# Where two joining copies of an encoder's FFN stand on ScalarE's queue: ahead of a weight cast, or behind it

## The chip, the cores and the metric

The kernel runs on one core of a Trainium2 chip. The time is that of the whole program on the device in microseconds (us), the median of several executions. A core has a matrix engine (TensorE, PE), three engines for elementwise work (VectorE or DVE, ScalarE or ACT, GpSimd or POOL), and SyncE (SP), which issues most of the DMAs here. Each engine has its own list of instructions, and the lists are tied by semaphores.

## The reference

Two layers (`DEPTH`) work on 256 tokens of width 1024. Each layer has a mixing part (gated linear attention and grouped-query attention in parallel, merged and projected), a SwiGLU FFN, and a per-layer embedding. The change concerns the FFN alone:

```python
D_MODEL = 1024
SEQ = 256
FFN_HIDDEN = -(-8 * D_MODEL // (3 * 256)) * 256      # 2816
...
    gate, up = jnp.split(rms_norm(h, g_ffn_pre) @ w_ffn_in, 2, axis=-1)
    h = h + rms_norm((jax.nn.silu(gate) * up) @ w_ffn_out, g_ffn_post)

    e = p_i @ w_ple_proj
    h = h + rms_norm(jax.nn.sigmoid(h @ w_ple_gate) * e, g_ple_post)
```

All inputs are float32.

## The kernel before, in words

**Precision.** A float32 matrix product is made of three products in the type fp32r: each operand is split into a high part (a cast on ScalarE) and a low part (the rest, a subtraction on VectorE). `split` (L135) issues both, the cast first. So every weight that TensorE uses costs a ScalarE cast and a VectorE subtraction, in two halves of 128x1024 each, and VectorE's half needs ScalarE's.

**Weights.** `Stream` (the object `ws`) brings the weights, in units of 128x2048 float32. SP's queue issues a load (L298) into a buffer `raw_…` (there are two), the split goes into a pair `wh_…`, `wl_…` (four of each), and TensorE frees a pair with the last matmul that reads it. `put` cuts a unit into two halves; `fill` splits ordinary units, `made` those of a pair (below).

**The order of the FFN.** The hidden 2816 columns are 11 blocks of 256. The first block is done by halves of the tokens; three (`PLAIN`, 4, 5 and 10) are done plainly; three pairs of blocks (`PAIRS` = 2, 6, 8) are done by seven products in place of eight (`seven`, with the weight sums of `step` on VectorE in buffers called `lent_…`). A string says in which order the parts come: u is half a plain block, 1 to 7 are the products of a pair, o is one step of the projection back (`out_step`), p loads a gain:

```python
FFN = "uu12u34u5u67" "uo12o34o5o67" "poo12o345o67"
PLAIN, PAIRS = (4, 5, 10), (2, 6, 8)
OUT = (0, 1, 2, 3, 4, 5, 10, 6, 7, 8, 9)
```

TensorE's order follows this string. The steps behind it (`out_step` for the eleven blocks, the product with the embedding's gate) make up the layer's end.

**Turning the hidden activations.** The projection back needs them with the hidden index on the partitions. `turned` does this as a task in the background for each half of the tokens (`hf` 0 or 1) of the first block and of each pair, and once for a plain block. `turn_out` (L456) copies the two 16-bit planes of the activations apart on ScalarE (L461 or L466) and has SP issue a transposing DMA (L467); some matmuls later, `take_in` (L470) joins the planes with a copy on ScalarE (L474, the "joining copy", a tile `mid_…` from a tile `t_…`) and splits the result into `hid` (a tile `big_…`): a joining cast on ScalarE and a joining low part on VectorE. The last pair is turned on TensorE instead.

**Who sets the order on the queues.** A scheduler gives each engine its list; work from a piece of code that stands earlier has priority, and `tc.high_priority(AHEAD)` lifts some of it. `tc.issue_after(x.ins)` holds what is issued in it behind the instruction `x`. Before the change, `take_in` used it for one copy alone: that of (k, hf) = (0, 0), behind the copy apart of (0, 1).

**The other neighbours.** `gain` (L373) loads a gain row for all partitions through SP, `up_weights` (L828 to L832) loads and casts the small decay weights of the next layer, and in `seven` the copies L738, L741 and L745 take products from PSUM.

Of the kernel before, what the change touches and what calls it, by code (L numbers as in the profile page):

```python
# [43 lines left out]
PLAIN, PAIRS = (4, 5, 10), (2, 6, 8)  # L44
# [17 lines left out]
def trunk_kernel(ctx: ExitStack, tc: tile.TileContext, a: dict, out: bass.AP):  # L62
# [28 lines left out]
    def mid(dt=F32):  # L91
        return b4p.tile([P, 1024], dt, tag="mid", name=nm("mid"))
# [40 lines left out]
    def split(hi, lo, src):  # L133

        return nc.scalar.copy(hi, src), nc.vector.tensor_tensor(out=lo, in0=src, in1=hi.bitcast(F32), op=ALU.subtract)  # L135
# [99 lines left out]
    class Load:  # L235


        def __init__(self, make, own=None, waits=False):
            self.make, self.own, self.waits, self.raw, self.n = make, own, waits, None, 0
# [8 lines left out]
    class Stream:  # L248
# [7 lines left out]

        def __init__(self, depth):
            self.depth, self.held, self.room, self.ready, self.open = depth, 0, 0, [], False
            self.loads, self.jobs, self.lend, self.last = [], [], False, {}
            pairs = {}  # L260
            for item in plan:
                if callable(item):
                    x = Load(item)
                    self.loads.append(x)
                    self.jobs.append(lambda x=x: self.plain(x))
                else:
                    units, n = item
                    if n == 1:
                        b11, b12, b21, b22 = units
                        x, z = (Load(b, lambda tag=tag: self.lent(tag), tag == "wh") for b, tag in ((b11, "wh"), (b12, "wl")))  # L270
                        y, q = Load(b22, big), Load(b21)
                        pairs[id(units)] = x, y, z, q
                        self.loads += [x, y, z]
                    if n == 5:
                        self.loads.append(q)
                    self.jobs.append(lambda p=pairs[id(units)], n=n: self.step(n, *p))
# [41 lines left out]

        def made(self, x):
            for piece in self.put(x):  # L320
                split(*piece)

        def step(self, n, x, y, z, q):
            c = slice(0, 2048)
# [22 lines left out]
        def fill(self):  # L347
            while self.open and self.held < self.depth and self.jobs:
                n = self.total - len(self.jobs)
                pieces = self.jobs.pop(0)()  # L350
                for piece in pieces or ():
                    self.last[n] = split(*piece)
                if pieces:
                    self.load()

# [12 lines left out]
    ws = Stream(4)  # L368
# [77 lines left out]
    def transpose_in(sp, src, k, n, hf, plain=None):  # L446

        ps = aux()
        for i in range(n):
            nc.tensor.transpose(ps[:, i * P : (i + 1) * P], src[:, i * P : (i + 1) * P], ident)  # L450
        with tc.high_priority(AHEAD):
            sp.put(ps[:, : n * P], k, n, hf * P, P)
        if plain is not None:
            nc.scalar.copy(plain, ps[:, : n * P])

    def turn_out(src, parts, mixed=False):  # L456

        with tc.high_priority(AHEAD):
            planes, words = (t.bitcast(U16) for t in (parts, src))
            if mixed:  # L460
                apart = nc.scalar.copy(  # L461
                    planes.rearrange("p (s k h f) -> p s k h f", s=2, k=2, f=P),
                    words.rearrange("p (h k f s) -> p s k h f", h=2, f=P, s=2),
                )
            else:
                apart = nc.scalar.copy(planes.rearrange("p (s c) -> p s c", s=2), words.rearrange("p (c s) -> p s c", s=2))  # L466
        nc.sync.dma_start_transpose(out=words.rearrange("p (x t) -> p x t", t=P), in_=planes)  # L467
        return apart

    def take_in(hi, lo, src, parts, behind=None):  # L470

        tn = hi.shape[-1]
        with tc.issue_after(behind.ins) if behind is not None else nullcontext():
            nc.scalar.copy(  # L474
                parts.bitcast(U16).rearrange("p (k t s) -> p k t s", s=2, t=tn),
                src.bitcast(U16).rearrange("p (s k t) -> p k t s", s=2, t=tn),
            )
        split(hi, lo, parts.rearrange("p (k t) -> p k t", t=tn))

    last_pow = [None]  # L480

# [62 lines left out]
    def halves(t):  # L544
        return [t[:, j * 512 : (j + 1) * 512] for j in range(2)]
# [140 lines left out]
    def sums(x):  # L686

        made = []

        def make():
            yield 1
            (a11, a12), (a21, a22) = x() if callable(x) else x
            s2 = t512()
            vsub(a22, a21, a22)
            vsub(s2, a11, a22)
            vsub(a12, a12, s2)  # L700
            yield 1
            vsub(a21, a21, a11)
            for s in (a12, a22, a21, s2):
                parts = halves(mid(F32R))
                split(*parts, s)
                made.append([p.rearrange("p (k t) -> p k t", t=P) for p in parts])
                yield 1

        return made, Task(make(), part[0])

    def seven(sp, forms, gated, alone=()):

        made, task = forms
        quad = lambda hf, j: lambda k: sp.tok(4 * j + k, hf)
        form = lambda i: lambda k: [p[:, k, :] for p in made[i]]
# [286 lines left out]
    def keep_embedding():  # L1002

        made = next(embedding)
        kept = keptp.tile([P, 2, D], F32, tag="kept", name=nm("kept"))
        nc.sync.dma_start(kept, made)
        return kept
# [39 lines left out]
    for l in range(DEPTH):  # L1047
# [249 lines left out]
        for x in range(2):  # L1297
            for i, o in enumerate(project_t(uT)):
                dst, r = qk[:, x, i, :], 1.0 if x else P**-0.5
# [142 lines left out]
        for j in range(2):  # L1442
            o = project(uT)
            for hf in range(2):
                dst = gg[:, hf, j * 512 : (j + 1) * 512]
# [3 lines left out]
        def out_gate():  # L1449
            while not (gla.over and attention.over):  # L1450
                yield 1
            for hf in range(2):
                sg = mid()
                with tc.issue_after(last_exp[0].ins):
                    nc.scalar.activation(sg, gg[:, hf, :], AF.Sigmoid)
                for j, t in enumerate(halves(sg)):
                    s = slice(j * 512, (j + 1) * 512)
                    vmul(t, t, gg[:, hf, s])
                    vmul(t, t, on[:, hf, s])
                xs = [(t, gg[:, hf, j * 512 : (j + 1) * 512]) for j, t in enumerate(halves(sg))]  # L1460
                for x in xs:
                    turn_out(*x)

                def turn(hf=hf, xs=xs):
                    for j, x in enumerate(xs):
                        yield WAIT_GATED[hf] if j == 0 else 1
                        take_in(*gT.at(4 * j, 4, hf * P, P), *x)

                gT.makers[hf].append(Task(turn(), part[0]))
# [107 lines left out]
        hid, spare, apart = Split(), [], {}  # L1577
        us = [[ws.take() for _ in range(2)] for _ in range(2)]

        def turned(src, k, hf):  # L1580

            def turn():
                if k == 2 * PAIRS[-1]:
                    yield WAIT_LAST[hf]
                    transpose_in(hid, src, k, 4, hf)
                else:
                    if not spare:
                        spare.extend(halves(mid()))
                    parts = spare.pop()
                    apart[k, hf] = turn_out(src, parts, hf is None)  # L1590
                    yield WAIT_TURNED
                    while (k, hf) == (0, 0) and (0, 1) not in apart:
                        yield 1
                    dst = hid.at(k, 2, 0, T) if hf is None else hid.at(k, 4, hf * P, P)
                    take_in(*dst, src, parts, apart[0, 1] if (k, hf) == (0, 0) else None)

            t = Task(turn(), part[0], k // 4)
            for i in range(2) if hf is None else (hf,):
                hid.makers[i].append(t)
# [66 lines left out]
        for x in FFN:  # L1666
# [3 lines left out]
            if x == "o":  # L1670
                n, w = outs.pop(0), ws.take()
# [117 lines left out]
```

## Time and profile before

| | |
|---|---|
| median of 3 runs | 910.29 us (908.7, 910.29, 912.39) |
| profiled execution's own time | 908.97 us |
| span of its trace | 907.2 us |
| mean granted TensorE clock | 0.997 |
| busy share of the span: TensorE, VectorE, ScalarE, GpSimd | 99%, 87%, 70%, 11% |
| moved by DMA | 180.25 MB, mean 199 GB/s |
| chain that ended last, by engine | PE 71%, DVE 14%, DMA 7%, issue 3%, ACT 3% |

The span runs from the first instruction to the last; 1.8 us of the execution's own time lie around it. In the rows that follow in this document, a timeline line has the start in us from the span's start, the length in us, the engine, the kernel's line, the operation, the tiles (written <- read, buffer numbers left out), the shape, and a count where like instructions follow each other; in square brackets stands how long the engine idled just before, and what ended that. A tile called `0ffnin` belongs to layer 0's FFN, `1ffnin` to layer 1's.

Layer 0's FFN has its first block's second turning near 285 us and the second pair's near 382 us of the span; in layer 1 the second pair's is near 830 us.

### The profile page before, as it was taken

What the parts mean: (1) busy time and instruction counts of PE and PEld (TensorE: products, weight loads), DVE (VectorE), ACT (ScalarE), POOL (GpSimd) and SP (SyncE); (2) the same over time, 40 slices, a digit from 0 to 9 for tenths busy, and PEclk for the clock granted to TensorE, in tenths of its full rate; (3) what the DMA queues carried; (4) which work ended last, traced back from release to release, by engine and by line L of the source; (5) the groups of instructions that cost most, each with busy time, mean ns of one, the idle gap of its engine ahead of it and who ended that gap; (6) DMA issues with size and microseconds to landing.
All of it is one profiled execution on the core that took longest, in us unless ns stands there. A gap on an engine that the chain in (4) does not pass through costs nothing.

```text
span 907.2 us, 12121 instructions
## 1 busy us (share of the span) xinstructions
PE 896.5 (99%) x4447; PEld 758.1 (84%) x4447; DVE 791.2 (87%) x1021; ACT 635.3 (70%) x1027; POOL 103.6 (11%) x157
## 2 busy tenths in 40 slices
PE   9999999999999999999999999999999999999997
PEld 8898888878888888877898888888888888888786
DVE  7999989987769989898779899799877799999984
ACT  6688679664569686666676687697645796958563
POOL 3700221300100000000244001110001000000001
PEclk9999999999999999999999999999999999999998
DMA  8654449657497685947575524475574966858461
GB/s 284 219 189 137 140 140 241 212 185 235 139 300 197 211 252 179 285 140 258 183 281 191 182 93 140 139 231 179 193 233 132 312 179 200 249 212 242 144 244 47
DMA packets 116967, 180.25 MB, mean 199 GB/s; under 512 B 30942, under 2 KB 55014, under 8 KB 116396
## 3 DMA queue, kind: packets, MB, share of 16 engines
q1 hardware_dynamic: 116748, 179.35, 61.4%
q8 instruction: 35, 0.57, 0.3%
q14 instruction: 24, 0.20, 0.1%
q10 hardware_dynamic: 160, 0.14, 0.0%
HBM read 169.50 MB, written 3.15 MB: 190 GB/s over the span
## 4 chain that ended last, share of the span: by engine, by line
PE 71%; DVE 14%; DMA 7%; issue 3%; ACT 3%; POOL 0%; POOLq 0%; SPq 0%; ACTq 0%; DVEq 0%
PE acc_1ffnin L123 10%; PE acc_1gate L123 7%; PE acc_0ffnin L123 5%; DVE wl_0ffnin L135 5%; PE acc_1ffnin L107 5%; DVE wl_0gate L135 3%; PE acc_1rq L123 3%; PE acc_0gqk L107 2%; PE acc_1gqk L107 2%; PE acc_1wout L123 2%; PE acc_0ple L123 2%; PE acc_1gg L123 2%; PE acc_1v L123 2%; PE acc_0v L123 2%; PE acc_1merge L123 2%
## 5 line engine op out<-in xcount | busy, mean ns | idle before, releaser
L135 ACT CAST wh_1ffnin<-raw_1ffnin 128x1024 fp32r<-128x1024 f32 x38 | 38.3, 1049 | 21.7 <-DMA raw_1ffnin<-in_w_ffn_out_dram 7.2
L135 DVE TENSOR_TENSOR wl_0ffnin<-raw_0ffnin,wh_0ffnin 128x1024 fp32r<-128x1024 f32 x38 | 44.7, 1221 | 8.5 <-ACT wh_0ffnin L135 8.4
L135 ACT CAST wh_0ffnin<-raw_0ffnin 128x1024 fp32r<-128x1024 f32 x38 | 38.0, 1047 | 19.6 <-DMA raw_0ffnin<-in_w_ffn_out_dram 11.1
L135 DVE TENSOR_TENSOR wl_1ffnin<-raw_1ffnin,wh_1ffnin 128x1024 fp32r<-128x1024 f32 x38 | 44.9, 1220 | 7.6 <-ACT wh_1ffnin L135 7.5
L107 PE MATMUL acc_0ffnin<-wh_0ffnin,big_0ffnin 128*128 128x512 f32 x176 | 45.4, 392 | 0.5 <-DVE big_0ffnin L135 0.5
L107 PE MATMUL acc_1ffnin<-wh_1ffnin,big_1ffnin 128*128 128x512 f32 x176 | 45.2, 390 | 0.0
L123 PE MATMUL acc_1ffnin<-wh_1ffnin,big_1wout 128*128 128x512 f32 x168 | 41.5, 389 | 0.0
L123 PE MATMUL acc_0ffnin<-wh_0ffnin,big_0wout 128*128 128x512 f32 x168 | 41.5, 389 | 0.0
L107 PEld LDWEIGHTS acc_0ffnin<-wh_0ffnin,big_0ffnin 128*128 128x128 f32 x176 | 32.7, 188 | 8.1 <-DVE big_0ffnin L135 0.9
L107 PEld LDWEIGHTS acc_1ffnin<-wh_1ffnin,big_1ffnin 128*128 128x128 f32 x176 | 33.0, 188 | 7.0
L123 PEld LDWEIGHTS acc_1ffnin<-wh_1ffnin,big_1wout 128*128 128x128 f32 x168 | 31.5, 188 | 6.6
L123 PEld LDWEIGHTS acc_0ffnin<-wh_0ffnin,big_0wout 128*128 128x128 f32 x168 | 31.5, 188 | 6.5
L135 DVE TENSOR_TENSOR wl_0ffnin<-lent_0ffnin,wh_0ffnin 128x1024 fp32r<-128x1024 f32 x30 | 35.7, 1220 | 0.6 <-ACT wh_0ffnin L135 0.6
L135 DVE TENSOR_TENSOR wl_1ffnin<-lent_1ffnin,wh_1ffnin 128x1024 fp32r<-128x1024 f32 x30 | 35.6, 1217 | 0.0
L135 ACT CAST wh_1ffnin<-lent_1ffnin 128x1024 fp32r<-128x1024 f32 x30 | 30.3, 1051 | 4.6 <-DVE lent_1ffnin L333 1.5
L135 ACT CAST wh_0ffnin<-lent_0ffnin 128x1024 fp32r<-128x1024 f32 x30 | 30.3, 1050 | 4.4 <-PE acc_0ffnin L123 1.6
L135 DVE TENSOR_TENSOR wl_0gate<-raw_0gate,wh_0gate 128x1024 fp32r<-128x1024 f32 x20 | 24.0, 1246 | 7.9 <-ACT wh_0gate L135 7.9
L135 DVE TENSOR_TENSOR wl_1gate<-raw_1gate,wh_1gate 128x1024 fp32r<-128x1024 f32 x20 | 23.6, 1220 | 7.3 <-ACT wh_1gate L135 7.3
L135 ACT CAST wh_0gate<-raw_0gate 128x1024 fp32r<-128x1024 f32 x20 | 19.8, 1046 | 12.8 <-DMA raw_0gate<-in_w_o_gla_dram 6.7
L135 ACT CAST wh_1gate<-raw_1gate 128x1024 fp32r<-128x1024 f32 x20 | 19.9, 1049 | 11.3 <-DMA raw_1gate<-in_w_o_gla_dram 4.7
L107 PE MATMUL acc_0ffnin<-wl_0ffnin,big_0ffnin 128*128 128x512 f32 x88 | 25.4, 399 | 1.4 <-DVE wl_0ffnin L135 1.4
L107 PE MATMUL acc_1ffnin<-wl_1ffnin,big_1ffnin 128*128 128x512 f32 x88 | 24.5, 395 | 0.6 <-DVE wl_1ffnin L135 0.6
(730 smaller groups left out, 2739.5 us busy)
## 6 DMA issues: line engine op xcount, KB each, us to landing
raw_0ffnin<-in_w_ffn_out_dram SPq DMA_DIRECT2D x11, 1024.0 KB, 6.4
raw_1ffnin<-in_w_ffn_out_dram SPq DMA_DIRECT2D x11, 1024.0 KB, 6.3
lent_0ffnin<-in_w_ffn_in_dram SPq DMA_DIRECT2D x6, 1024.0 KB
lent_1ffnin<-in_w_ffn_in_dram SPq DMA_DIRECT2D x6, 1024.0 KB, 9.0
raw_0v<-in_w_in_dram SPq DMA_DIRECT2D x4, 1024.0 KB, 5.1
raw_0gate<-in_w_o_gla_dram SPq DMA_DIRECT2D x4, 1024.0 KB, 5.9
raw_0gate<-in_w_o_attn_dram SPq DMA_DIRECT2D x4, 1024.0 KB, 5.0
raw_0wout<-in_w_ffn_in_dram SPq DMA_DIRECT2D x8, 512.0 KB, 6.3
```

The source lines that it names most:

```text
L107: return nc.tensor.matmul(o, lhsT, rhs, start=start, stop=stop)
L123: nc.tensor.matmul(o, x, y, start=start and n == 0, stop=stop and n == len(seq) - 1, **kw)
L135: return nc.scalar.copy(hi, src), nc.vector.tensor_tensor(out=lo, in0=src, in1=hi.bitcast(F32), op=ALU.subtract)
```

## The change

`Stream` now remembers the last weight split that it issued (`self.cast`, the pair of the cast and the low part). `take_in` takes a tuple of instructions and holds the joining copy **and** its split behind all of them. For the first block's second half, (k, hf) = (0, 1), and for both halves of the second pair (k = 12), these are the cast and the low part of the last weight half that was issued; the copy of (0, 0) keeps its old place, with its split now bound too.

```diff
@@ class Stream
-            self.loads, self.jobs, self.lend, self.last = [], [], False, {}
+            self.loads, self.jobs, self.lend, self.last, self.cast = [], [], False, {}, None
...
         def made(self, x):
             for piece in self.put(x):
-                split(*piece)
+                self.cast = split(*piece)
...
                 for piece in pieces or ():
-                    self.last[n] = split(*piece)
+                    self.last[n] = self.cast = split(*piece)
...
-    def take_in(hi, lo, src, parts, behind=None):
+    def take_in(hi, lo, src, parts, behind=()):
 
         tn = hi.shape[-1]
-        with tc.issue_after(behind.ins) if behind is not None else nullcontext():
+        with ExitStack() as order:
+            for x in behind:
+                order.enter_context(tc.issue_after(x.ins))
             nc.scalar.copy(
                 parts.bitcast(U16).rearrange("p (k t s) -> p k t s", s=2, t=tn),
                 src.bitcast(U16).rearrange("p (s k t) -> p k t s", s=2, t=tn),
             )
-        split(hi, lo, parts.rearrange("p (k t) -> p k t", t=tn))
+            split(hi, lo, parts.rearrange("p (k t) -> p k t", t=tn))
...
                     dst = hid.at(k, 2, 0, T) if hf is None else hid.at(k, 4, hf * P, P)
-                    take_in(*dst, src, parts, apart[0, 1] if (k, hf) == (0, 0) else None)
+                    late = (k, hf) == (0, 1) or k == 2 * PAIRS[1]
+                    take_in(*dst, src, parts, ws.cast if late else (apart[0, 1],) if (k, hf) == (0, 0) else ())
```

No instruction is added or taken out, and the lists of TensorE, VectorE and GpSimd stay as they were. ScalarE's list changes at two places in each layer, SP's at one in layer 0. Lines behind L470 have numbers higher by 2 or 3 in the changed kernel (the joining copy is L476).

ScalarE, layer 0, where the second pair is joined: `mid_0ffnin_3463<-t_0ffnin_3460` is the joining copy of the pair's second half, `wh_0ffnin_3534` the next weight's high part, `big_0ffnin_3524` the turned activations, `wh_0ffnin_3562` the weight after that. Before:

```order
L474 COPY mid_0ffnin_3155<-t_0ffnin_3434 128x1024
L135 CAST big_0ffnin_3524<-mid_0ffnin_3155 128x4x128
L474 COPY mid_0ffnin_3463<-t_0ffnin_3460 128x1024
L135 CAST wh_0ffnin_3534<-raw_0ffnin_3396 128x1024 x2
L135 CAST big_0ffnin_3524<-mid_0ffnin_3463 128x4x128
L738 COPY mid_0ffnin_3542<-acc_0ffnin_3544 128x512
L135 CAST wh_0ffnin_3562<-lent_0ffnin_3390 128x1024 x2
```

The same place after the change:

```order
L476 COPY mid_0ffnin_3155<-t_0ffnin_3434 128x1024
L135 CAST big_0ffnin_3524<-mid_0ffnin_3155 128x4x128
L135 CAST wh_0ffnin_3534<-raw_0ffnin_3396 128x1024 x2
L476 COPY mid_0ffnin_3463<-t_0ffnin_3460 128x1024
L740 COPY mid_0ffnin_3542<-acc_0ffnin_3544 128x512
L135 CAST big_0ffnin_3524<-mid_0ffnin_3463 128x4x128
L135 CAST wh_0ffnin_3562<-lent_0ffnin_3390 128x1024 x2
```

Both halves of the weight's cast now stand ahead of the joining copy, and the copy from PSUM (L740) ahead of the joining cast. In layer 1 the same rows move in the same way.

ScalarE, layer 0, where the first block's second half is joined: `mid_0ffnin_2657<-t_0ffnin_2660` is the joining copy, `wh_0ffnin_2834` and `wh_0ffnin_2862` are the next two weights' high parts, L1628 is the activation of a plain block, L461 its copy apart, L738 and L741 copies from PSUM. Before:

```order
L135 CAST wh_0ffnin_2796<-big_0ffnin_2690 128x1024 x2
L474 COPY mid_0ffnin_2657<-t_0ffnin_2660 128x1024
L1628 ACTIVATE t_0ffnin_2762<-acc_0ffnin_2763 128x256
L135 CAST big_0ffnin_2771<-mid_0ffnin_2657 128x4x128
L135 CAST wh_0ffnin_2834<-raw_0ffnin_2700 128x1024
L1628 ACTIVATE t_0ffnin_2762<-acc_0ffnin_2764 128x256
L135 CAST wh_0ffnin_2834<-raw_0ffnin_2700 128x1024
L135 CAST wh_0ffnin_2862<-lent_0ffnin_2688 128x1024 x2
L461 COPY mid_0ffnin_2831<-t_0ffnin_2762 128x1024
L738 COPY mid_0ffnin_2842<-acc_0ffnin_2844 128x512
L135 CAST wh_0ffnin_2883<-lent_0ffnin_2692 128x1024
L741 COPY mid_0ffnin_2843<-acc_0ffnin_2869 128x512
```

After:

```order
L135 CAST wh_0ffnin_2796<-big_0ffnin_2690 128x1024 x2
L1631 ACTIVATE t_0ffnin_2762<-acc_0ffnin_2763 128x256
L135 CAST wh_0ffnin_2834<-raw_0ffnin_2700 128x1024
L1631 ACTIVATE t_0ffnin_2762<-acc_0ffnin_2764 128x256
L135 CAST wh_0ffnin_2834<-raw_0ffnin_2700 128x1024
L476 COPY mid_0ffnin_2657<-t_0ffnin_2660 128x1024
L135 CAST wh_0ffnin_2862<-lent_0ffnin_2688 128x1024
L461 COPY mid_0ffnin_2831<-t_0ffnin_2762 128x1024
L135 CAST big_0ffnin_2771<-mid_0ffnin_2657 128x4x128
L740 COPY mid_0ffnin_2842<-acc_0ffnin_2844 128x512
L135 CAST wh_0ffnin_2862<-lent_0ffnin_2688 128x1024
L743 COPY mid_0ffnin_2843<-acc_0ffnin_2869 128x512
```

The joining copy and its cast went behind both halves of one weight's cast, and the joining cast and two other copies (L461, L740) now stand ahead of the second half of the weight after that.

SP, layer 0, the last loads of the FFN stage: `raw_…` are buffers for weights, `mid_0ffnout_3783` takes the gain `g_ple_post`, `mid_0ffnin_3772` the small decay weights of layer 1. Before:

```order
L829 DMA mid_0ffnin_3772<-in_b_alpha_dram 1x1024
L298 DMA raw_0ffnin_3639<-in_w_ffn_out_dram 128x2x1024
L298 DMA raw_0ffnin_3677<-in_w_ffn_out_dram 128x2x1024
L373 DMA mid_0ffnout_3783<-in_g_ple_post_dram 128x1024
L298 DMA raw_0ffnin_3691<-in_w_ffn_out_dram 128x2x1024
```

After:

```order
L831 DMA mid_0ffnin_3772<-in_b_alpha_dram 1x1024
L373 DMA mid_0ffnout_3783<-in_g_ple_post_dram 128x1024
L298 DMA raw_0ffnin_3639<-in_w_ffn_out_dram 128x2x1024
L298 DMA raw_0ffnin_3677<-in_w_ffn_out_dram 128x2x1024
L298 DMA raw_0ffnin_3691<-in_w_ffn_out_dram 128x2x1024
```

The gain's load moved ahead of two weight loads; it writes a buffer that the joining low part of the second pair reads last. On ScalarE the cast of the small decay weights (L832) likewise moved ahead of the cast of one weight (`wh_0ffnin_3679`).

## The prediction

> **What bounds the kernel now.** I read the page first: TensorE is busy nearly all the span.
>
> ```profile
> PE 896.5 (99%) x4447; PEld 758.1 (84%) x4447; DVE 791.2 (87%) x1021; ACT 635.3 (70%) x1027; POOL 103.6 (11%) x157
> ```
>
> A reordering on ScalarE can therefore bring only what TensorE loses while it waits, and cost only by making it wait more. So the second view was TensorE's timeline around the moved copies, read by starts (columns: start, length, engine, line, instruction, tiles). Layer 0, the joining of the second pair:
>
> ```profile
> 378.87 1.07 PE L107 MATMUL acc_0ffnin<-wh_0ffnin,big_0ffnin 128*128 128x512 f32 x4
> 379.78 1.98 PE L123 MATMUL acc_0ffnin<-wh_0ffnin,big_0wout 128*128 128x512 f32 x8
> ...
> 386.16 0.63 PE L107 MATMUL acc_0ffnin<-wl_0ffnin,big_0ffnin 128*128 128x512 f32 x2
> 387.04 0.74 PE L107 MATMUL acc_0ffnin<-wl_0ffnin,big_0ffnin 128*128 128x512 f32 x2 [0.25 <-DVE wl_0ffnin L135]
> 387.61 1.99 PE L107 MATMUL acc_0ffnin<-wh_0ffnin,big_0ffnin 128*128 128x512 f32 x8
> ...
> 399.41 1.07 PE L107 MATMUL acc_0ffnin<-wh_0ffnin,big_0ffnin 128*128 128x512 f32 x4
> 400.74 0.73 PE L107 MATMUL acc_0ffnin<-wl_0ffnin,big_0ffnin 128*128 128x512 f32 x2 [0.26 <-DVE wl_0ffnin L135]
> 401.87 0.73 PE L107 MATMUL acc_0ffnin<-wl_0ffnin,big_0ffnin 128*128 128x512 f32 x2 [0.40 <-DVE wl_0ffnin L135]
> 402.44 1.99 PE L107 MATMUL acc_0ffnin<-wh_0ffnin,big_0ffnin 128*128 128x512 f32 x8
> ```
>
> Four matmuls without a wait take 379.78 - 378.87 = 0.91 us. From 386.16 to 387.61 four took 1.45: 0.54 lost. From 399.41 to 402.44 eight took 3.03 instead of 1.82: 1.21 lost. All wait for a low part (wl) that VectorE makes. Then ScalarE and VectorE, to see why those are late:
>
> ```profile
> 374.96 7.49 DMA t_0ffnin<-mid_0ffnin
> ```
> ```profile
> 382.47 1.17 ACT L474 COPY mid_0ffnin<-t_0ffnin 128x1024 uint16<-128x1024 uint16 x1 [2.67 <-DMA t_0ffnin<-mid_0ffnin]
> 383.55 2.00 ACT L135 CAST wh_0ffnin<-raw_0ffnin 128x1024 fp32r<-128x1024 f32 x2
> 385.45 0.61 ACT L135 CAST big_0ffnin<-mid_0ffnin 128x512 fp32r<-128x512 f32 x1
> ...
> 386.44 2.00 ACT L135 CAST wh_0ffnin<-lent_0ffnin 128x1024 fp32r<-128x1024 f32 x2
> ```
> ```profile
> 381.70 0.68 DVE L135 TENSOR_TENSOR big_0ffnin<-mid_0ffnin,big_0ffnin 128x512 fp32r<-128x512 f32 x1
> 384.62 2.36 DVE L135 TENSOR_TENSOR wl_0ffnin<-raw_0ffnin,wh_0ffnin 128x1024 fp32r<-128x1024 f32 x2 [2.23 <-ACT wh_0ffnin L135]
> 386.90 0.69 DVE L135 TENSOR_TENSOR big_0ffnin<-mid_0ffnin,big_0ffnin 128x512 fp32r<-128x512 f32 x1
> 387.52 2.36 DVE L135 TENSOR_TENSOR wl_0ffnin<-lent_0ffnin,wh_0ffnin 128x1024 fp32r<-128x1024 f32 x2
> ...
> 399.46 4.62 DVE L135 TENSOR_TENSOR wl_0ffnin<-raw_0ffnin,wh_0ffnin 128x1024 fp32r<-128x1024 f32 x4
> ```
> ```profile
> 390.00:405.00 15.00, 14.34 (x63) 11.23 (x62) 15.00 (x13) 10.05 (x11) 0.00 (x0) 1.00 0.28 90
> ```
>
> The chain (first fence) goes through the transposing DMA. ScalarE stands at the joining copy until 382.47; the weight cast at 383.55 is behind it, though its weight is there; VectorE idles 2.23 us for that cast, and after 387.52 it has no gap left (busy 15.00 of 15.00 us in the last row), so the delay reaches 399.46 and TensorE at 400.74.
>
> **The second pair in layer 0.** The cast now stands ahead of the copy. It needs the buffer that TensorE reads in the row at 378.87 until about 379.9, so it starts near 380.0 and its halves end by 382.0, inside the old wait. The copy still starts at 382.47. Behind it come the small copy from PSUM and the joining cast: by the spacing of the rows (1.08 from 382.47 to 383.55; 0.99 for the two from 385.45 to 386.44), they end near 384.6. No instruction is added.
>
> VectorE keeps its order: low parts from 382.3 (behind 381.70) to 384.6, the joining half's low part at 384.67, then the low part of the next weight, whose first cast half runs 384.54 to 385.6. It starts at 385.63 instead of 387.52: 1.89 us earlier. The 2.23 do not come whole, since VectorE now waits some 0.1 for the joining cast and 0.3 for the next weight cast. The Trainium skill, page "PSUM — Partial Sum Buffer", section "Engine vs sequencer instructions", has these engines' queues as strict FIFO; by that rule the joining half cannot be passed, as in the rows; if it could, the sum would be 0.3 to 0.4 larger at this place.
>
> With 1.89 us less, the low parts of 399.46 end at 398.8 and 399.9. TensorE, 0.54 ahead, wants them at 399.8 and 400.2. Both stalls go, 0.54 + 1.21 = 1.75 us, with 0.3 us to spare at the last.
>
> What is late next is the end of this FFN stage:
>
> ```profile
> 415.64 1.16 PE L107 MATMUL acc_0ffnin<-wl_0ffnin,big_0ffnin 128*128 128x512 f32 x4
> 417.26 1.20 PE L107 MATMUL acc_0ffnin<-wh_0ffnin,big_0ffnin 128*128 128x512 f32 x4 [0.47 <-DVE big_0ffnin L135]
> ...
> 419.78 0.63 PE L107 MATMUL acc_0ffnin<-wl_0ffnin,big_0ffnin 128*128 128x512 f32 x2
> 420.67 0.73 PE L107 MATMUL acc_0ffnin<-wl_0ffnin,big_0ffnin 128*128 128x512 f32 x2 [0.26 <-DVE wl_0ffnin L135]
> 421.24 2.01 PE L107 MATMUL acc_0ffnin<-wh_0ffnin,big_0ffnin 128*128 128x512 f32 x8
> ```
> ```profile
> 408.33 2.00 ACT L135 CAST wh_0ffnin<-raw_0ffnin 128x1024 fp32r<-128x1024 f32 x2 [5.72 <-DMA raw_0ffnin<-in_w_ffn_out_dram]
> ```
> ```profile
> DMA to landing us min/median/max: 6.5/6.5/6.5
> ```
> ```profile
> DMA to landing us min/median/max: 5.2/5.2/5.2
> ```
>
> Here TensorE loses 417.26 - 415.64 - 0.91 = 0.71 and 421.24 - 419.78 - 0.91 = 0.55. Both hang on a VectorE run that begins with the weight cast at 408.33, which waits for a load; that load is issued when VectorE has done the low parts of 399.46, so 1.89 earlier. If it takes as long as before, VectorE is 1.89 ahead, TensorE 1.75, and the stalls shrink by 0.14 only. But the change also moves the load of a gain (in_g_ple_post) on SP's queue from behind the two weight loads to ahead of them, where it waits only for the joining half's low part (near 385.4) and is gone long before. The two landing lines are for the w_ffn_out loads issued in the stretch 398 to 415 (layer 0, the gain among them) and 846 to 858 (layer 1, the same place and no gain near): 6.5 and 5.2. After the change layer 0 stands as layer 1 does, so between these ends I take 5.2. That is 1.3 more for VectorE than TensorE has gained, against stalls of 0.71 + 0.55 = 1.26. Layer 0 then gains 1.75 + 1.26 = 3.0; the lower end is 1.89.
>
> The page "DMA: Bandwidth & Descriptors" of the Trainium skill, section "Queues, rings and completion order", says that descriptors on each DMA engine are consumed in ring order. By that rule a gain issued behind the weight load should hold it little, the 6.5 has another cause and stays, and layer 0 gains 1.9; no run here separates the two, and this is a rival below.
>
> Also moved there: the cast of the small alpha weights now stands ahead of one weight cast; that gives ScalarE 1 us of work earlier in a stretch where it is busy 10.05 of 15.00 us, so I cost it at nothing; without that cover it costs 1.0.
>
> **The second pair in layer 1.**
>
> ```profile
> 829.98 1.18 ACT L474 COPY mid_1ffnin<-t_1ffnin 128x1024 uint16<-128x1024 uint16 x1 [2.83 <-DMA t_1ffnin<-mid_1ffnin]
> ```
> ```profile
> 832.14 2.36 DVE L135 TENSOR_TENSOR wl_1ffnin<-raw_1ffnin,wh_1ffnin 128x1024 fp32r<-128x1024 f32 x2 [1.17 <-ACT wh_1ffnin L135]
> ```
> ```profile
> 847.03 1.07 PE L107 MATMUL acc_1ffnin<-wh_1ffnin,big_1ffnin 128*128 128x512 f32 x4
> ...
> 849.39 0.73 PE L107 MATMUL acc_1ffnin<-wl_1ffnin,big_1ffnin 128*128 128x512 f32 x2 [0.40 <-DVE wl_1ffnin L135]
> 849.96 2.01 PE L107 MATMUL acc_1ffnin<-wh_1ffnin,big_1ffnin 128*128 128x512 f32 x8
> ```
>
> The same picture, smaller: VectorE idles 1.17, TensorE takes 2.93 for eight matmuls, 1.11 lost. The cast fits into ScalarE's 2.83 us wait, and VectorE comes 1.17 earlier. The last low part, ready just before 849.39, is then ready near 848.2; TensorE unhindered wants it at 848.4. The whole 1.11 goes, with 0.2 to spare. No stall follows in this layer that could take it back.
>
> **The first group's second half, both layers.**
>
> ```profile
> 284.07 1.98 PE L123 MATMUL acc_0ffnin<-wh_0ffnin,big_0wout 128*128 128x512 f32 x8
> ```
> ```profile
> 285.27 1.17 ACT L474 COPY mid_0ffnin<-t_0ffnin 128x1024 uint16<-128x1024 uint16 x1 [1.73 <-DMA t_0ffnin<-mid_0ffnin]
> ...
> 293.57 0.60 ACT L741 COPY mid_0ffnin<-acc_0ffnin 128x512 f32<-128x512 f32 x1
> ```
> ```profile
> 289.70 2.35 DVE L135 TENSOR_TENSOR wl_0ffnin<-raw_0ffnin,wh_0ffnin 128x1024 fp32r<-128x1024 f32 x2
> ...
> 293.70 2.36 DVE L135 TENSOR_TENSOR wl_0ffnin<-lent_0ffnin,wh_0ffnin 128x1024 fp32r<-128x1024 f32 x2
> ```
>
> TensorE has no gap here, so there is nothing to win; the question is what it costs. The weight cast that goes ahead needs a buffer that TensorE frees at 284.07 + 1.98 = 286.05. From there ScalarE has nearly the work it did from 285.27 to 293.57 (8.30 us; one small activation, 0.27, is done earlier, and the copy at 293.57, 0.48, comes before instead of after): the first half of the fourth weight's cast ends at about 294.7. VectorE takes it up in the second instruction of the row at 293.70, at 294.84. So zero, with 0.13 us of cover; a slip x beyond it would reach TensorE as x in layer 0, where VectorE's chain is on the critical chain, bounded by the 1.6 us that copy and joining cast take. I take 0.
>
> **Sum.** 3.0 + 1.1 + 0 = 4.1 us off the profiled execution's own 908.97: 904.9. The median of the runs before, 910.29, lies 1.32 higher, and on that scale it is 906.2.
>
> **Rivals.** (1) The raw load takes 6.5 again: 1.89 + 1.11 = 3.0, so 907.3. For it: the ring order, and the load sits 2.3 us ahead of its neighbours; against: layer 1's 5.2.
>
> (2) VectorE gets no lead: the low parts are held by their own next wait (joining half, lent weight) or by a transposing DMA that lands later in other executions, and only the first stall goes: 0.54, so 909.8. Against it: the spare of 0.2 to 0.3 us would have to be missed in both layers.
>
> (3) Slower: "behind the low part" becomes a real wait of ScalarE for VectorE, not only a place in its queue. At the first group the copy would then start after the low parts of 289.70 end, at 292.05, not near 288.3: 3.8 us in which every cast behind it stands. From a hold of 0.13 us on, layer 0 pays: 3.7 us. Layer 1 pays up to as much, say half for want of a stall there. The pair gains nothing, as its joining copy would start at 384.7. Together 5.6: 915.9. Against it: the built instruction has as its one wait the DMA's semaphore.
>
> **How the numbers follow.** Forecast 0.45, (1) 0.32, (2) 0.13, (3) 0.10. About 0.5% (4.55 us) is what a measurement of this kernel can tell from no change. The forecast is 0.45 short of that, and the three runs before spread from 1.6 below to 2.1 above their median, so a third of it falls beyond: 0.15, and 0.03 of (1): faster 0.18. Slower takes most of (3) and a little noise: 0.09. The rest, 0.73, is same. The range goes from 1.9 below the forecast (904.3) to (2) with the lower of those two spreads, 1.6, on top (911.4).
>
> **What would show it.** Right: no TensorE wait for VectorE in the two places of the second pair; VectorE's idle before the weight's low parts at 384.62 and 832.14 gone, and a short one (0.1) ahead of the joining half instead; the load for the cast at 408.33 landing in 5.2, and the stalls of 417.26 and 420.67 gone. Landing in 6.5 with those two stalls there says (1). A ScalarE wait for VectorE at the joining copy says (3). The forecast is wrong if TensorE's losses elsewhere, for example ahead of 340 in layer 0, grow.

## The result and the profile after

Twelve runs of each kernel gave 906.18 us after (904.33 to 907.7) against 910.32 before (906.48 to 912.39): a ratio of 0.9963, 95% interval 0.9949 to 0.9977, so 3.4 us less, give or take 1.3. The profiled execution after took 905.83 with a span of 903.9; that of before, 908.97.

TensorE's row of the page and its timeline where the second pair is joined in layer 0:

```profile
PE 893.8 (99%) x4447; PEld 759.2 (84%) x4447; DVE 791.5 (88%) x1021; ACT 636.2 (70%) x1027; POOL 102.1 (11%) x157
```
```profile
385.83 1.07 PE L107 MATMUL acc_0ffnin<-wl_0ffnin,big_0ffnin 128*128 128x512 f32 x4
386.74 1.98 PE L107 MATMUL acc_0ffnin<-wh_0ffnin,big_0ffnin 128*128 128x512 f32 x8
...
398.52 1.07 PE L107 MATMUL acc_0ffnin<-wh_0ffnin,big_0ffnin 128*128 128x512 f32 x4
399.43 1.07 PE L107 MATMUL acc_0ffnin<-wl_0ffnin,big_0ffnin 128*128 128x512 f32 x4
400.34 1.98 PE L107 MATMUL acc_0ffnin<-wh_0ffnin,big_0ffnin 128*128 128x512 f32 x8
...
415.69 1.17 PE L107 MATMUL acc_0ffnin<-wh_0ffnin,big_0ffnin 128*128 128x512 f32 x4
416.70 1.08 PE L107 MATMUL acc_0ffnin<-wl_0ffnin,big_0ffnin 128*128 128x512 f32 x4
...
419.43 1.07 PE L107 MATMUL acc_0ffnin<-wl_0ffnin,big_0ffnin 128*128 128x512 f32 x4
420.34 1.98 PE L107 MATMUL acc_0ffnin<-wh_0ffnin,big_0ffnin 128*128 128x512 f32 x8
...
437.55 0.66 PE L1022 MATMUL aux_1emb<-ident,mid_0ffnout 128*128 128x128 f32 x4 [1.08 <-DMA mid_0ffnout<-in_p_dram]
```

No row has a wait in brackets until 437.55, and groups of four follow one another every 0.91 us (1.01 at 415.69): the waits that before's TensorE had here are gone. A new wait of 1.08 us stands at 437.55, for the small load of p. ScalarE and VectorE at the joining:

```profile
379.68 2.01 ACT L135 CAST wh_0ffnin<-raw_0ffnin 128x1024 fp32r<-128x1024 f32 x2 [1.67 <-PE acc_0ffnin L107]
381.59 1.16 ACT L476 COPY mid_0ffnin<-t_0ffnin 128x1024 uint16<-128x1024 uint16 x1
```
```profile
381.18 2.35 DVE L135 TENSOR_TENSOR wl_0ffnin<-raw_0ffnin,wh_0ffnin 128x1024 fp32r<-128x1024 f32 x2
383.80 0.69 DVE L135 TENSOR_TENSOR big_0ffnin<-mid_0ffnin,big_0ffnin 128x512 fp32r<-128x512 f32 x1 [0.27 <-ACT big_0ffnin L135]
384.75 2.36 DVE L135 TENSOR_TENSOR wl_0ffnin<-lent_0ffnin,wh_0ffnin 128x1024 fp32r<-128x1024 f32 x2 [0.26 <-ACT wh_0ffnin L135]
```

The cast fills what was ScalarE's wait, the copy finds its DMA landed, and VectorE waits 0.27 and 0.26 us where it had waited 2.23. Then the weight load at the end of the stage (SyncE's issues, before's first and then the changed kernel's, and the changed kernel's cast that waits for the first of them) and layer 1's place:

```profile
401.85 2.65 SPq L298 DMA_DIRECT2D raw_0ffnin<-in_w_ffn_out_dram  x2
```
```profile
399.11 9.07 SPq L298 DMA_DIRECT2D raw_0ffnin<-in_w_ffn_out_dram  x3
```
```profile
404.34 2.00 ACT L135 CAST wh_0ffnin<-raw_0ffnin 128x1024 fp32r<-128x1024 f32 x2 [3.91 <-DVE mid_0ffnin L720]
```
```profile
844.92 1.07 PE L107 MATMUL acc_1ffnin<-wh_1ffnin,big_1ffnin 128*128 128x512 f32 x4
845.83 1.07 PE L107 MATMUL acc_1ffnin<-wl_1ffnin,big_1ffnin 128*128 128x512 f32 x4
846.74 1.98 PE L107 MATMUL acc_1ffnin<-wh_1ffnin,big_1ffnin 128*128 128x512 f32 x8
```

The cast starts 404.34 - 399.11 = 5.23 us after the issue of its load; before it was 408.33 - 401.85 = 6.48. Layer 1 has no stall left either.

Matmul by matmul, TensorE's starts after against before (times on before's span): 0.6 gained at 387, 1.24 at 400 to 402, 1.65 from 412 to 432, 1.27 given back at 437, 1.15 gained at 847; together 3.37 of the span's 3.3. Other differences cancel within a microsecond and are of one execution (-0.5 at 340, +0.5 at 707).

### The profile page after: what moved, and what is told of

Read it like the earlier page. It is cut to its first block, busy times and chain, and to the rows that moved or that the text cites. A ratio compares the mean times of both kernels' runs of the same rounds, so it can differ in the third digit from the quotient of the medians.

```text
span 903.9 us, 12119 instructions
## 1 busy us (share of the span) xinstructions
PE 893.8 (99%) x4447; PEld 759.2 (84%) x4447; DVE 791.5 (88%) x1021; ACT 636.2 (70%) x1027; POOL 102.1 (11%) x157
## 4 chain that ended last, share of the span: by engine, by line
PE 79%; DVE 9%; DMA 6%; ACT 3%; issue 2%; POOL 1%; SPq 0%; POOLq 0%; ACTq 0%; DVEq 0%
PE acc_1ffnin L123 11%; PE acc_0ffnin L123 10%; PE acc_1gate L123 7%; PE acc_1ffnin L107 7%; PE acc_0ffnin L107 4%; PE acc_1rq L123 3%; PE acc_0gqk L107 2%; PE acc_1gqk L107 2%; DVE wl_0gate L135 2%; PE acc_1v L123 2%; PE acc_1gg L123 2%; PE acc_0v L123 2%; PE acc_1merge L123 2%; PE acc_1ple L123 2%; PE acc_0wout L123 2%
```

## The experiments

Each was timed beside the kernel before on the same chip; its profile is one execution, so a wait there shows a mechanism, and the ratio its worth.

**Which part works.** Two kernels delay only one of the two places:

```
-                    late = (k, hf) == (0, 1) or k == 2 * PAIRS[1]
+                    late = k == 2 * PAIRS[1]          # pair_only
+                    late = (k, hf) == (0, 1)          # first_only
```

> Only the second pair's joining copies go behind the weight cast; the first block's second half is joined as before. Theory (the pair alone brings the gain, the first block's place is worth nothing): 906.2 us, that is 4.1 below the kernel before (0.9955 of it), no TensorE wait for VectorE in the two places of the second pair. Rival (the first block's place brings part of it, by a lead that VectorE keeps until the stall near 340 us): 0.4 to 1.0 us longer, 906.6 to 907.2, with that stall back. Rival (the first block's place costs, its cover of 0.13 us being overrun): shorter, 905.5.

> Only the first block's second half goes behind the weight cast; the second pair is joined as before, and the gain's load stands again behind the two weight loads. Theory: 910.3 us, the time of the kernel before within 0.5 us (ratio 0.9995 to 1.0005); VectorE's work near 290 to 306 us without a new gap, all stalls of 387 to 421 us and of 848 us there. Rival (the first block's place brings part of the gain): 909.3 to 909.9. Rival (it costs): 910.8 to 912.

The pair alone took 907.57 us, 0.9971 of before (0.9951 to 0.9991); the first group alone 908.94, 0.9986 (0.9966 to 1.0005), no clear difference. TensorE's timeline of the pair alone and then of the first group alone:

```profile
437.72 0.66 PE L1022 MATMUL aux_1emb<-ident,mid_0ffnout 128*128 128x128 f32 x4 [0.76 <-DMA mid_0ffnout<-in_p_dram]
```
```profile
399.80 0.73 PE L107 MATMUL acc_0ffnin<-wl_0ffnin,big_0ffnin 128*128 128x512 f32 x2 [0.26 <-DVE wl_0ffnin L135]
400.93 0.73 PE L107 MATMUL acc_0ffnin<-wl_0ffnin,big_0ffnin 128*128 128x512 f32 x2 [0.40 <-DVE wl_0ffnin L135]
```

With the pair moved, TensorE has no stall in the FFN stage and the new wait at 437 comes; the span is the 903.9 of the whole change. With the first group moved, the old stalls at 400 and 401 are there. The gain comes with the pair, and the first group's edit has no effect that these runs can measure. (The stall at 387 is down from 0.6 to 0.4 us in the first group's profile too; what varies there comes below.)

**The two layers apart.**

```
+                    late = l == 0 and k == 2 * PAIRS[1]     # pair_l0
+                    late = l == 1 and k == 2 * PAIRS[1]     # pair_l1
```

> Only layer 0's second pair is joined late; layer 1's and the first blocks are as before. Theory: layer 0's stalls from 387 to 421 us go (3.0 us), about 1.0 us is given back at 437 us, where TensorE comes sooner to a transpose whose load lands no sooner: 2.0 us less than before, 907.8 us; layer 1's stalls of 848 and 849 us are there. Rival (nothing is given back, the wait at 437 us is chance): 3.0 us less, 906.8. Rival (the layers' gains don't add, layer 1's part is the larger): 909.3 or more.

> Only layer 1's second pair is joined late. Theory: 1.1 us less than before, 908.7 us; TensorE's two waits near 848 and 849 us are gone, layer 0's from 387 to 421 us are there. Rival (something else in layer 1 takes it back): 909.8. Rival (layer 1's part is the larger): 907.5 or less.

Layer 0 alone took 906.80, 0.9982 (0.9964 to 1.0); layer 1 alone 909.42, 0.9994 (0.998 to 1.0009). TensorE in layer 0 alone, then in layer 1 alone:

```profile
436.58 0.60 PE L1022 MATMUL aux_1emb<-ident,mid_0ffnout 128*128 128x128 f32 x4
...
846.21 0.73 PE L107 MATMUL acc_1ffnin<-wl_1ffnin,big_1ffnin 128*128 128x512 f32 x2 [0.25 <-DVE wl_1ffnin L135]
847.35 0.73 PE L107 MATMUL acc_1ffnin<-wl_1ffnin,big_1ffnin 128*128 128x512 f32 x2 [0.40 <-DVE wl_1ffnin L135]
```
```profile
398.85 1.11 PE L107 MATMUL acc_0ffnin<-wl_0ffnin,big_0ffnin 128*128 128x512 f32 x4
...
414.67 1.19 PE L107 MATMUL acc_0ffnin<-wh_0ffnin,big_0ffnin 128*128 128x512 f32 x4 [0.47 <-DVE big_0ffnin L135]
...
418.07 0.73 PE L107 MATMUL acc_0ffnin<-wl_0ffnin,big_0ffnin 128*128 128x512 f32 x2 [0.25 <-DVE wl_0ffnin L135]
```

The moved layer loses its stalls in both kernels. The layer left alone keeps its own only in part: layer 1's two are there in the first kernel, but in the second layer 0 has the two at the end of its stage and not the two that the forecast of 1.75 us was read from. Its four matmuls from 398.85 take 0.95 us, with the pair joined as before; VectorE idled 0.93 us for the weight cast there, not 2.23. Those two stalls are thus not in every execution of the "old order", that is, with this pair joined as in the kernel before. In time neither alone stands clear of no change, and layer 1 by itself (0.5 us, from 1.8 less to 0.8 more) is compatible with the 1.1 us of its stalls but does not prove them. The new wait at 437 is absent in the first kernel, though layer 0's stalls are gone there too, so it does not follow from them alone.

**The gain's load.** The prediction laid the 6.5 us landing to the load of the gain behind it. One kernel is the changed one with the gain issued behind the two weight loads again; the other is the kernel before with the gain issued two weight loads later.

```
         gple = gain(a["g_ple_post"][l], mid(), D)        # both, in layer 0, under:
+        with tc.issue_after(ws.sent[-5].ins):            # gain_behind, on the changed kernel
+        with tc.issue_after(ws.sent[-3].ins):            # before_gain_later, on the kernel before
```

> The changed kernel with one load moved back: layer 0's g_ple_post gain is issued behind the two weight loads of w_ffn_out, where it stood before; all else is as in the changed kernel. Theory (the gain's load lengthened the weight load's landing from 5.2 to 6.5 us): the weight load lands in 6.5 again, the two stalls at the end of layer 0's FFN (0.71 and 0.55 us) return in part or whole, 907.0 to 907.5 us. Rival (the landing has another cause, such as the neighbouring weight load's distance, which the earlier low parts changed): landing 5.2, no stalls, 906.2.

> The kernel before with one load moved: layer 0's g_ple_post gain is issued two weight loads later, away from the landing that took 6.5 us; ScalarE's order is that of the kernel before. Theory (the gain's load lengthened the landing): it lands in 5.2 us, the stalls of 0.71 and 0.55 us at the end of layer 0's FFN go, 1.0 to 1.3 us less than before: 909.0 to 909.3 us. Rival (another cause): landing 6.5, both stalls there, 910.3.

The first took 906.03, 0.9959 (0.994 to 0.9978), like the whole change; the second 909.04, 0.9983 (0.9965 to 1.0002). SyncE's issues and ScalarE's cast of the first, then of the second, with TensorE's stall there:

```profile
399.63 2.66 SPq L298 DMA_DIRECT2D raw_0ffnin<-in_w_ffn_out_dram  x2
402.33 0.47 SPq L373 DMA_DIRECT2D mid_0ffnout<-in_g_ple_post_dram  x1
```
```profile
404.68 2.01 ACT L135 CAST wh_0ffnin<-raw_0ffnin 128x1024 fp32r<-128x1024 f32 x2 [3.73 <-PE acc_0ffnin L107]
```
```profile
401.16 10.45 SPq L298 DMA_DIRECT2D raw_0ffnin<-in_w_ffn_out_dram  x3
```
```profile
407.77 2.01 ACT L135 CAST wh_0ffnin<-raw_0ffnin 128x1024 fp32r<-128x1024 f32 x2 [5.85 <-DMA raw_0ffnin<-in_w_ffn_out_dram]
```
```profile
416.71 1.19 PE L107 MATMUL acc_0ffnin<-wh_0ffnin,big_0ffnin 128*128 128x512 f32 x4 [0.46 <-DVE big_0ffnin L135]
```

With the gain back behind the loads the cast comes 5.05 us after the issue; with the gain away it comes 6.61 after. The late landing follows the gain in neither kernel: this step of the prediction is refuted.

**What does lengthen the load.** A load ends with sixteen packets of 4 bytes. In the profile of before fifteen of them came between 406.07 and 406.26, and the last at 407.10, when one packet of 16 KB of queue q8, which started at 406.20 and took 0.92 us, came to its end. The records do not say which of the sixteen DMA engines a packet ran on; that these two shared one is read from the times. The Trainium skill, page "DMA: Bandwidth & Descriptors", section "Why a DMA increments its semaphore by 16 and not by 1", says that the engines of a DMA finish independently, each raising the semaphore at its end, and that only all sixteen mean landed; the trace agrees, with sixteen steps of the semaphore, the last at 6.38 us from the issue, and the cast at 6.48. The DMA queues of before from the load's issue to its last packet (packets, MB, share):

```profile
q1 hardware_dynamic: 379, 1.49, 71.8%
q8 instruction: 1, 0.02, 1.1%
```

In the changed kernel a q8 packet starts at 403.64, when the load is all but done: the load's last small packet comes at 403.75. There are 35 such packets in a span, one in some 127 matmuls. The page "Runtime: NRT & Kernel Launch" of the Trainium skill, section "Instruction fetch mechanics", has instructions fetched in blocks of 16 KiB, 256 of them, and calls the cost of the crossing "mostly hidden". Size and number agree (4447 matmuls with a weight load each, by 256, is 34.7). The cost looked for here is another one, that of a load in flight beside the fetch. To test it, two kernels give TensorE 52 more instructions in its warm-up (26 more narrow matmuls, 37 of 32 columns for 11 of 128), which moves its later fetches and leaves the order of all else as it was:

```
-        warm_up(WARM[2])
+        for _ in range(WARM[2] + 26):      # fetch_before, fetch_after
+            on("pe", mm, warm[:, 0:32], seed, seed[:, 0:32], True, True)
```

> The kernel before, with TensorE's third row of warming matmuls at the start made of 37 narrow ones (32 columns) in place of 11 of 128 columns: 52 more instructions, so that each fetch of TensorE's instructions (a 16 KB packet every 127 matmuls or so) falls some 6 us earlier in the program; the order of all else is as before. Theory (the weight load near 402 us lands in 6.5 us because such a packet holds one of its DMA engines for 0.9 us): the packet comes near 400 us, ahead of the load, the load lands in 5.1 to 5.4, the two stalls near 417 and 420 us shrink by 0.6 to 1.2 us together; the time as a whole by as much, if no other load is hit: 908.6 to 909.2. Rival (the load's landing has nothing to do with the packet): 6.0 to 6.7 again and both stalls there, 909.8.

> The changed kernel with the same 52 additional instructions at TensorE's start, so that the packet of instructions near 430.4 us comes near 424 us instead, away from the load of p that TensorE waits for at 437 us. Theory (that packet makes p land late): the wait of 0.9 to 1.2 us at 437 us goes, 905.2 us if no other load is hit. Rival (p lands late for another reason, such as the weight load issued 0.4 us ahead of it): the wait is there again, 906.2.

On the kernel before (nine runs): 906.49, 0.9967 (0.9952 to 0.9982). On the changed kernel (six runs): 904.21, 0.9947 (0.9933 to 0.9962), the best version. Both came out faster than their theory said. The first one's load issues, cast, and queues over the load:

```profile
400.08 2.66 SPq L298 DMA_DIRECT2D raw_0ffnin<-in_w_ffn_out_dram  x2
```
```profile
405.27 2.00 ACT L135 CAST wh_0ffnin<-raw_0ffnin 128x1024 fp32r<-128x1024 f32 x2 [4.43 <-DVE mid_0ffnin L718]
```
```profile
q1 hardware_dynamic: 355, 1.39, 73.3%
```

Only TensorE's list was edited, and the packets moved from 406.2 to 396.2 and from 403.6 to 394.2: q8 is its queue here. No q8 packet lies over the load now, and the unmoved kernel's cast comes 5.19 us after the issue, as in the changed one. The load is not all that changed, though: this profile of the old order has no stall in layer 1 either, so its 3.0 us cannot all be put down to the one load. The changed kernel's TensorE loses the wait at 437 and has losses of 2.2 us from 680 to 700 in its place, one of them this wait of 1.03 us:

```profile
435.24 0.60 PE L1023 MATMUL aux_1emb<-ident,mid_0ffnout 128*128 128x128 f32 x4
...
680.56 0.50 PE L123 MATMUL acc_1wout<-wh_1merge,big_1merge 128*128 128x512 f32 x1 [1.03 <-ACT big_1merge L135]
```

**The packets back over the load.** With 26 more instructions the packets fall over the load in both kernels. The first pair of kernels (24 matmuls of 32 columns) went wrong in another way:

```
+        for _ in range(WARM[2] + 13):      # fetch13_before, fetch13_after: 0:32
+            on("pe", mm, warm[:, 0:32], seed, seed[:, 0:32], True, True)
+            on("pe", mm, warm[:, 0:58], seed, seed[:, 0:58], True, True)   # fetch13w_...: 0:58 instead
```

> A control for fetch_before: the kernel before with 26 additional instructions at TensorE's start in place of 52 (24 matmuls of 32 columns for the 11 of 128), so that the packet of instructions moves half as far, to about 401 to 404 us, which is inside the flight of the weight load issued near 401 us. Theory (the packet's place among the loads is what counts): the load lands in 5.9 to 6.7 us, the stalls near 417 and 420 us are there (0.6 to 1.2 us together), and the time is 907.5 to 909.5 us, 1.0 us or more above fetch_before. Rival (the additional narrow matmuls bring the gain in themselves, wherever the packets fall): landing 5.1 to 5.4, 906.5 us.

> The same control on the changed kernel: 26 additional instructions, the packet near 398 to 401 us, at the start of the weight load issued near 399 us, and the next one near 427 us, ahead of the load of p. Theory: the weight load lands later than the 5.1 us of the changed kernel where the packet falls into its flight (5.7 to 6.4 us), no wait at 437 us; 905 to 906.5 us in all. Rival (the additional matmuls themselves): 904.2 us.

911.43, 1.003 (1.0013 to 1.0047), and 910.55, 1.0011 (0.9997 to 1.0025). They lost 2.45 and 2.2 us in the first microseconds, so they decide nothing about the load's worth; the same two were run with 58 columns in a row.

> fetch13_before again with its 24 warming matmuls 58 columns wide in place of 32, so that they last as long as the 11 of 128 columns did; in fetch13_before TensorE's first matmuls after them ran at half pace and cost 2.4 us. Theory (the packet's place counts): the start costs 0.5 us at most, the packet falls near 401 us, into the flight of the weight load issued near 400 us, which lands in 5.7 to 6.7 us; 908.5 to 910 us in all. Rival (26 more instructions help wherever the packets fall, as in fetch_before): 906.5.

> fetch13_after with its 24 warming matmuls 58 columns wide, for the same reason. Theory (what the change brings depends on where the packets of instructions fall): the start costs 0.5 us at most; the packet near 400 us falls into the flight of the weight load issued near 399 us, the stalls near 417 and 420 us come back in part, and the time is 906.5 to 908.5 us, above the changed kernel's own 906.2. Rival (26 more instructions help wherever the packets fall): 904.2.

911.17, 1.0032 (1.0009 to 1.0054), and 909.12, 0.999 (0.9977 to 1.0004). On the kernel before, the first eight real matmuls with 32 columns, with 58, and, with 58, a stall of the FFN stage:

```profile
5.10 2.61 PE L107 MATMUL acc_0rq<-wh_start,big_start 128*128 128x288 f32 x8 [0.49 <-ACT wh_start L144]
```
```profile
5.13 1.49 PE L107 MATMUL acc_0rq<-wh_start,big_start 128*128 128x288 f32 x8
...
417.90 0.74 PE L107 MATMUL acc_0ffnin<-wl_0ffnin,big_0ffnin 128*128 128x512 f32 x2 [0.26 <-DVE wl_0ffnin L135]
```

And the changed kernel's load with 58 columns: issue, cast, queues over it:

```profile
401.43 2.65 SPq L298 DMA_DIRECT2D raw_0ffnin<-in_w_ffn_out_dram  x2
```
```profile
407.39 2.00 ACT L135 CAST wh_0ffnin<-raw_0ffnin 128x1024 fp32r<-128x1024 f32 x2 [4.65 <-DMA raw_0ffnin<-in_w_ffn_out_dram]
```
```profile
q1 hardware_dynamic: 377, 1.48, 76.0%
q8 instruction: 1, 0.02, 1.6%
```

The same code that had 5.23 us now takes 5.96, with the packet over the load. In the changed kernel with 58 columns the first eight matmuls took 2.12 us, so its start lost 1.0 us, more than the 0.5 allowed. The load came late in all four kernels, as the theory said, but both times with 58 columns lie above the theory's range, so the place of this packet does not account for the whole time.

All fourteen profiles together (us; packet, last of the sixteen and cast counted from the load's issue). The two columns of losses are TensorE's time between the same two matmuls, those that start in before near 378 and 405 us, and near 413 and 434, less the shortest of the fourteen:

| kernel | q8 packet at | last of 16 | cast | second pair in layer 0 | lost 378 to 405 | lost 413 to 434 |
|---|---|---|---|---|---|---|
| before | 4.35 | 5.25 | 6.48 | as before | 1.8 | 2.0 |
| first_only | 1.04 | 5.30 | 5.95 | as before | 1.6 | 1.4 |
| before_gain_later | 3.81 | 6.04 | 6.61 | as before | 0.4 | 2.0 |
| pair_l1 | 3.51 | 5.88 | 6.51 | as before | 0.1 | 2.0 |
| fetch13_before / fetch13w_before | 0.90 / 1.14 | 5.44 / 5.21 | 6.08 / 5.77 | as before | 0 / 0 | 1.2 / 1.0 |
| fetch13_after / fetch13w_after | 1.21 / 0.92 | 5.55 / 5.34 | 6.14 / 5.96 | moved | 0 / 0 | 1.2 / 1.3 |
| fetch_before | none | 4.70 | 5.19 | as before | 0.5 | 0.7 |
| fetch_after | none | 4.45 | 5.05 | moved | 0 | 0.1 |
| after | 4.53 | 4.64 | 5.23 | moved | 0 | 0.3 |
| pair_only / gain_behind / pair_l0 | 4.39 / 4.39 / 4.41 | 4.44 / 4.39 / 4.43 | 5.06 / 5.05 / 5.00 | moved | 0 / 0 / 0 | 0.3 / 0 / 0.2 |

A packet inside the flight goes with 5.8 to 6.6 us, none or one at its very end with at most 5.2, in all fourteen, wherever the gain and the pair stand. The losses at the end of the stage go with the cast, and the two kernels that have the pair moved and the packet inside the flight lose 1.2 to 1.3 us there. The losses from 378 to 405 are gone wherever the pair is moved; with the old order they run from nothing to 1.8.

In the change itself the load is issued 2.74 us earlier and the packet comes 2.56 earlier; by this account those 0.18 us, by which VectorE gained more than TensorE, let the load slip past. That step is argued and not shown: the border between "inside" (4.35) and "at the end" (4.39) is read from the outcomes themselves. And in before the cast came 1.23 us after the last small packet, where in the other thirteen it came 0.5 to 0.7 after, so some 0.6 of its 6.48 us has another cause, which stays open.

## Why the prediction was right, and where its steps failed

The time (906.2 forecast, 906.18 measured), the sign and the range held. Step by step:

- **The two stalls of the second pair in layer 0**: right between these two profiles, 1.75 forecast and 0.6 + 1.24 = 1.8 found, but not a steady cost of the old order. VectorE's lead was more than forecast: 387.52 - 384.75 less the 0.29 by which the two executions already differed is 2.48, not 1.89, since the copy started at 381.59 without waiting; the sum had kept the landing at 382.47. Where the pair is as before, VectorE's idle at this place varied from 0.90 to 2.23 us between profiles, and 2.23, on which the sum rests, is the largest. With 2.23 and 2.02 TensorE lost 1.8 and 1.6 us there, with 0.90 to 1.29 at most 0.5; over the four profiles of the old order with TensorE's original list the mean is 1.0.
- **The tail of that stage**: right in size by a wrong term. 1.26 forecast, 1.65 found. The cast did come 5.2 us after the issue and not 6.5, but not for the gain's load: the two gain experiments refute that term, and the fetch experiments put TensorE's instruction packets in its place. Rival 1 was right that the gain holds the load little, and wrong that 6.5 therefore stays. The two quoted landings moreover were of unlike loads: 6.5 was that of the second of layer 0's two loads, 5.2 that of the first of layer 1's. The cast at 408.33 waits for the first, and came 6.48 after its issue; the second still landed 6.71 us after its own issue in the changed kernel.
- **Layer 1**: right in the trace, 1.11 forecast and 1.15 found. These stalls are steadier than layer 0's: 0.8 to 1.3 us from 845 to 852 in six of the seven profiles that have layer 1's pair as before, nothing in the seventh (fetch_before). Their worth in time is not separately shown.
- **The first group at nothing**: right. The third cast's first half ended at 294.92 (start 293.86, and one such cast takes 1.06), and VectorE's third low part started at 295.05 (three take 3.49 from 292.78, one 1.22): the 0.13 us of cover are there to the digit. Rival 3 is refuted by the row at 381.59, where the copy follows its cast with no wait for VectorE, by the first group's copy, which starts at 288.47 while that weight's low parts start at 289.91, and by the pair-only kernel, which is no faster without the first group.
- **"The forecast is wrong if TensorE's losses elsewhere grow"**: one did. The wait at 437.55 takes back 1.27 of layer 0's gain. The sum had no such term; chance differences and the larger tail filled the gap. In the three profiles that have the wait (whole change, pair only, gain behind) a q8 packet comes at 430.4 to 430.7, 0.1 to 0.5 us after the load of p is issued, and p lands 7.0 to 7.6 us after its issue. In fetch_after the packet comes at 425.85, p lands in 5.8, and no wait stands there. But a packet also comes 0.5 to 0.7 us after the issue in layer 0 alone and in four kernels with the old order in layer 0, and there p lands in 5.7 to 5.9. So a packet close behind the issue is not enough to make p late, and the cause stays open.

So the number was partly luck. Over the profiles with the original list of TensorE, moving the pair shortens the stretch from 339 to 431 by 2.5 us on the mean (four with, four without; 3.0 forecast, from a profile of before that was the worst of its four) and the stretch from 828 to 858 by 1.8 (1.1 forecast). Of the 2.5 some 1.0 are the two stalls of the pair; the rest is the end of the stage, which goes with the packet. In time the change brings 3.4 us with the packets as they were, 906.49 - 904.21 = 2.3 with 52 more instructions, and with 26 more 911.43 - 910.55 = 0.9 (32 columns, both losing over 2 us at the start) and 911.17 - 909.12 = 2.05 (58 columns, where the changed kernel's profile loses 1.0 in the first microseconds and the other's 0.2). What the reordering does of itself lies between one and three and a half microseconds; how much of the 3.4 comes from where the packets fall, intervals of one to two microseconds each do not tell.

## What to carry to other kernels

A reordering is worth the stalls that end in the wait it covers, and four-matmul spacings size these well for the execution they are read from; but before a longer DMA is put down to its neighbour on the queue, look at the last of its sixteen closing packets and at what else was moving just ahead of it. When a tuned kernel's time moves by a few tenths of a per cent, run the change at two or three phases of TensorE's instruction stream before crediting it. A profile of one execution can be the worst of its kind, as here VectorE's 2.23 us and the 1.8 us of stalls behind it, which four of the six other profiles with the old order had at 0.4 us or less. So terms taken from one profile should be checked against a second one.

## What the runs showed of the hardware

- A 16 KB instruction packet took 0.88 to 1.9 us, where a 4 KB data packet takes 0.16 (the median in before), and the cast behind a megabyte load in flight then came up to 1.4 us later (6.61 against 5.19 after the issue). Moving these packets by 26 or 52 instructions took the changed kernel from 906.18 to 909.12 and 904.21 us, a spread of 4.9 (some 1.0 of it lost at the start in the profile of the first), where the change itself brought 3.4.
- 768 columns of narrow warm-up matmuls (24 of 32) left the first eight real matmuls at 2.61 us instead of 1.49, in both kernels, while the profile's granted clock read full. 37 of 32 columns gave 1.50 and 1.49; 24 × 58 = 1392 columns gave 1.49 in one kernel and 2.12 in the other, so the number of columns alone does not settle it.
- The transposing DMA of one pair left ScalarE waiting between 1.85 and 2.97 us in seven kernels that are the same there, and VectorE behind it between 0.90 and 2.23.
